# Memory keys loaded by tokens instead of by heads, in a hybrid decoder layer

## Chip, core and metric

The kernel runs on one core of a Trainium2 chip. The metric is the device time of one execution in microseconds (us), as the median of several runs. Beside it stands one execution taken by the hardware profiler, whose rows are read here. Engines are named as the profile names them: PE (matrix multiplications; PEld its weight loads), DVE (vector engine), ACT (scalar engine), POOL, and SP, which here only issues DMAs. DMAs are carried out by 16 DMA engines that all queues share.

## What is computed

One layer of a decoder serves a prompt of 512 tokens and, with the same weights, eight samples of four tokens each. Three sub-layers follow each other: a mixer (an mLSTM group and a differential-attention group), cross-attention into 256 memory tokens, and a gated MLP with a short convolution. The change lies in the cross-attention of the samples, whose keys and values come from a cache:

```
def mem_attend(h, mk, mv, w_mq, w_mo):
    B, T, _ = h.shape
    q = (h @ w_mq).reshape(B, T, MEM_HEADS, MEM_HEAD_DIM)
    s = jnp.einsum('bqhd,bkhd->bhqk', q.astype(jnp.float32), mk.astype(jnp.float32)) * (MEM_HEAD_DIM ** -0.5)
    p = jax.nn.softmax(s, axis=-1)
    o = jnp.einsum('bhqk,bkhd->bqhd', p, mv.astype(jnp.float32)).reshape(B, T, D_MODEL)
    return o.astype(h.dtype) @ w_mo
```

For the samples `mk` and `mv` are `cache_mem_k` and `cache_mem_v`, of shape (1, 8, 256, 4, 256): eight samples, 256 tokens, four heads of 256 numbers. In memory a token's four heads lie behind each other (4 KB), and one head of one token is a piece of 1 KB. Keys and values are 8.4 MB each, all in float32.

## The kernel before

The whole layer is one program for one core. A scheduler places the instructions of all engines by its own estimate of their times, and each engine then runs its instructions strictly in that order. Nearly all loads are issued by SP, one behind the other. Weights come in slots of a ring (`wslot`, tag `W`, four buffers) by way of a staging ring (`wst`, six buffers).

The stage around the change is the projection of queries with `w_mq` and the attention behind it:

- `gemmB(hqT, ...)` multiplies `w_mq` in eight column blocks. The first four run as two halves of columns (matmuls at L472), the last four block by block (L485). Each block ends with an evacuation from PSUM: ACT writes `qh` (L1420), DVE the rest `ql` (L1421), and ACT the samples' queries `qs` (L1423). Five PSUM buffers serve these products in turn.
- POOL spreads `qs` into `qx` (L1408), a matrix with the queries of one head in each row group.
- `mk_load(b)` loads the keys of sample b (L1493): two halves of 128 tokens, each into a tile of 128 partitions by 1024 columns. Partition 32 h + t holds head h; column 256 k + d holds number d of token 32 k + t. The tiles are staging buffers (`wst`) for three samples, weight slots (`kvt`, free when a block of the projection is done) for four, and one extra tile.
- `mk_turn(b)` transposes each tile in blocks of 32 by 32 on DVE (L1498), so that the head's dimension lies on partitions.
- `mk_scores` multiplies them with `qx` on PE (L1510), for the samples 0, 2, 4, 6 first and 1, 3, 5, 7 later, between pieces of the prompt's own cross-attention (L1441, L1459, L1471). The sums, the softmax and the values' product (`mv_out`, L1548) follow. The values are loaded (`mv_load`, L1538) into the buffers that the scores have given back.
- Behind that SP loads the convolution's rows (`cr`) and `w_mo`, and PE goes on with the output projection and the MLP.

At L1766 and L1767, in the MLP, a tile `cvr` is stored to two outputs. The prediction uses these stores for comparison: the first takes 8 partitions of 128 numbers to 2 rows with 4 blocks each, the second 64 partitions to 16 rows with 4 blocks each. At L1775 a store of 16 partitions goes to 16 rows.

Of the kernel before, what the change touches and what calls it, by code (L numbers as in the profile page):

```python
# [15 lines left out]
P = 128  # L16
# [4 lines left out]
NS = NB * TS  # L21
ROWS = SEQ + NS
H = 4
# [54 lines left out]
def kernel(ctx: ExitStack, tc: tile.TileContext, I, O):  # L78
# [29 lines left out]
    def T2(shape, name, dt=F32):  # L108
        return t2p.tile(list(shape), dt, name=name, tag="T2")
# [17 lines left out]
    def v2(t, b):  # L127
        return t.rearrange("p (a b) -> p a b", b=b)
# [10 lines left out]
    dma = nc.sync.dma_start  # L139
# [69 lines left out]
    def stage():  # L209
        return stg.tile([P, 1024], F32, name="wst", tag="st")  # L210
# [319 lines left out]
    for b in range(2):  # L530
        kept.append(norm_turn(xms[b], P, "g_mem_src", memT, b * P))
        if b == 0:

            t = turned[0].ins
            fill = mmp("fill")
            for _ in range(NFILL):
                with burst(t):
                    t = mm(fill, lhsT=warm[:, 0:P], rhs=warm, start=True, stop=True).ins
# [132 lines left out]
    for c0, c1 in HALF:  # L671
# [5 lines left out]
        t = T2([64, n], "gt")  # L677
# [253 lines left out]
    for g in range(2):  # L931
        for h in range(0, H, 2):
            t = stage().rearrange("p (j b e) -> p j b e", j=2, b=4)
# [38 lines left out]
    t = None  # L972
    for h in range(H):
        with burst(t):
            t = mm(pg[NS * h:NS * h + NS, P:2 * P + 1], lhsT=sm_t[:, h, :], rhs=vNs[:, h, :], start=True, stop=True).ins
    for h in range(H):
        with burst(t):
            t = mm(pg[NS * h:NS * h + NS, 4:12], lhsT=qT[:, h, SEQ:], rhs=nT[:, h, :], start=True, stop=True).ins
    for b in range(NB):
        for h in range(H):  # L980
            with burst(t):
                t = mm(pi[NS * h:NS * h + NS, 0:P], lhsT=qzm[:, 256 * h + b * NS:256 * h + (b + 1) * NS],
                       rhs=csts[b // 4, h][:, b % 4, :], start=(b == 0), stop=(b == NB - 1)).ins
# [226 lines left out]
    for b in range(4):  # L1210
        c = slice(b * P, b * P + P)
# [3 lines left out]
    kst, kts, pts, aTs, outs, rcs = {}, {}, {}, {}, {}, {}  # L1215
# [260 lines left out]
    kst, vts = {}, {}  # L1476
# [4 lines left out]
    def two(i):  # L1481

        if i < 3:
            return [stage(), stage()]
        t = wp.tile([P, 2, DM], F32, name="kvt", tag="W") if i < 7 else S([P, 2, DM], F32, "kvt")
        return [t[:, 0], t[:, 1]]

    def mk_load(b):

        kst[b] = two(home[b])  # L1490
        for c in range(2):
            for h in range(H):
                dma(out=v2(kst[b][c][NS * h:NS * h + NS], 256),  # L1493
                    in_=I["cache_mem_k"][0, b, c * P:(c + 1) * P, h].rearrange("(k t) d -> t k d", t=NS))

    def mk_turn(b):
        for t in kst[b]:
# [2 lines left out]
    def mk_scores(bs):  # L1500

        t = None
        for b in bs:
            ps = mmp("ssc")[:, :256]
            for c in range(2):
                kv = kst[b][c].rearrange("p (k j t) -> p k j t", j=8, t=NS)
                for j in range(8):
                    g = NS * (j % 4)
                    with burst(t):
                        t = mm(v2(ps[g:g + NS, c * P:c * P + P], NS), lhsT=qx[:, j, b // 2 * 2:b // 2 * 2 + 2].rearrange("p n r -> p (n r)"),  # L1510
                               rhs=kv[:, :, j, :], start=(j < 4), stop=(j >= 4)).ins
            nc.scalar.copy(out=sc[:, b], in_=ps)
        return t
# [40 lines left out]
    for k in range(4):  # L1554
        mk_load(SEQS[k])
    for i, _ in enumerate(gemmB(hqT, [ev_q(m) for m in range(4, 8)])):
        if i % 4 == 1:
            mk_turn(SEQS[i // 4])
        if i % 4 == 3:
            mk_load(SEQS[4 + i // 4])  # L1560
# [11 lines left out]
    t = mk_scores(SEQS[4:])  # L1572
# [205 lines left out]
    for gi, js in enumerate(groups):  # L1778
# [8 lines left out]
        def one(b, ps, i, s, cs=slice(0, 512)):  # L1787
            t = act[i // 2][:, i % 2]
            st, en = i == 0, i == nk - 1
            if b == 4:  # L1790
                return sample_mm(ps, [acs[i], acs[i + 1]], s[1], i == 0, i == nk - 2)
            s = s[0]
            c0 = b * P
            mm(ps, lhsT=t[:, 0, c0:c0 + P], rhs=s[:, 0, i % 2, cs], start=st, stop=False)  # L1794
            mm(ps, lhsT=t[:, 0, c0:c0 + P], rhs=s[:, 1, i % 2, cs], start=False, stop=False)  # L1795
            return mm(ps, lhsT=t[:, 1, c0:c0 + P], rhs=s[:, 0, i % 2, cs], start=False, stop=en)  # L1796
# [29 lines left out]
        if not last:  # L1826
            behind = []
            for n0 in (0, 512):
# [4 lines left out]
                for i in range(nk):  # L1833
# [3 lines left out]
                    for b in range(4):  # L1837
                        t = one(b, ps[b], i, s)
# [14 lines left out]
        def chunk(b, n0):  # L1853
            while len(wd) < (nk // 2 if n0 == 0 else nk):
                wd.append(W.get())
            w = 256 if (b, n0) == (TORD[-1], 512) else 512
            for o in range(0, 512, w):
                ps = mmp()[:, :w]
                for i in range(0, nk, 2 if b == 4 else 1):
                    t = one(b, ps, i, wd[(n0 and nk // 2) + i // 2], slice(o, o + w))  # L1860
                add_y(b, ps, n0 + o, w)
            return t
# [39 lines left out]
        t = chunk(TORD[1], 0)  # L1902

        for n0 in (0, 512):
            with burst(t.ins):
                t = chunk(TORD[0], n0)
# [78 lines left out]
```

## Time and profile before

| | |
|---|---|
| median of 3 runs | 952.89 us (952.66 to 952.95) |
| the profiled execution | 950.42 us |
| its span, first to last instruction | 948.6 us |
| mean granted clock of PE | 0.990 |
| PE busy | 918.3 us (97%) |
| DVE, ACT, POOL busy | 606.2, 377.7, 202.6 us |
| moved by DMA | 130.30 MB, 137 GB/s on average |

A row of a timeline has the start in us from the span's beginning, the duration, engine, line, operation, output and inputs with their shapes, the count of merged instructions, and in brackets the idle time of the engine before it and what ended it. A row of waits has who waited for whom, the total in us, how often, and the longest. The DMA share in a row by stretch is the mean busy share of the 16 DMA engines; transfers that were begun in a stretch count whole, so that it can exceed 1. PEclk is the clock that PE was granted, as a share of full speed.

### The profile page before, as it was taken

How to read it: one execution, taken by the hardware profiler on the slowest of the kernel's cores; microseconds unless marked ns; L12 is line 12 of the kernel's file. 1: busy time of each engine (PE TensorE's matmuls, PEld its weight loads, DVE VectorE, ACT ScalarE, POOL GpSimd, SP SyncE). 2: the span in 40 equal slices, each digit the busy share in tenths (PEclk: the TensorE clock that was granted, in tenths of full speed). 3: DMA queues.
4: the chain of work that ended last, by engine and by line, in shares of the span. 5: the costliest groups of instructions: out<-in, count | busy, mean ns of one | idle time of the engine just before them, and what ended most of it. 6: DMA issues, size and time to landing. Idle time of an engine off the chain costs nothing. (4 is left out here: it accounts for less than half of the span.)

```text
span 948.6 us, 17140 instructions
## 1 busy us (share of the span) xinstructions
PE 918.3 (97%) x6612; PEld 800.8 (84%) x6612; DVE 606.2 (64%) x1120; ACT 377.7 (40%) x727; POOL 202.6 (21%) x401
## 2 busy tenths in 40 slices
PE   8999999999999999988989999999999999999995
PEld 5899787889866778988767899989988997999974
DVE  6845145565886358576544778638757775676767
ACT  5655234344676357613434532322212222222232
POOL 6610000115432226301000544001110110110114
PEclk9999999999999999999989999999999999999998
DMA  8950023344870539999744733062053313512023
GB/s 285 309 183 2 2 88 137 89 139 131 280 245 9 176 103 343 262 192 260 273 175 124 208 126 89 25 174 72 8 142 100 102 27 92 153 49 89 24 93 116
DMA packets 127586, 130.30 MB, mean 137 GB/s; under 512 B 9336, under 2 KB 95193, under 8 KB 127505
## 3 DMA queue, kind: packets, MB, share of 16 engines
q1 hardware_dynamic: 121320, 125.70, 43.8%
q10 hardware_dynamic: 6184, 3.52, 1.2%
q8 instruction: 52, 0.85, 0.4%
q14 instruction: 30, 0.24, 0.1%
HBM read 112.26 MB, written 16.93 MB: 136 GB/s over the span
## 5 line engine op out<-in xcount | busy, mean ns | idle before, releaser
L485 PE MATMUL mm<-fT,wslot 128*128 128x256 f32 x1872 | 235.9, 288 | 0.0
L485 PEld LDWEIGHTS mm<-fT,wslot 128*128 128x128 f32 x1872 | 234.4, 188 | 1.8 <-issue 0.8
L146 ACT CAST wslot<-wst 128x1024 fp32r<-128x1024 f32 x125 | 130.7, 1050 | 256.7 <-issue 71.8
L147 DVE TENSOR_TENSOR wslot<-wst,wslot 128x1024 fp32r<-128x1024 f32 x125 | 155.2, 1246 | 83.3 <-ACT wslot L146 82.8
L1795 PE MATMUL mm<-wslot,act 128*128 128x512 f32 (+1 forms) x180 | 70.2, 391 | 0.0
L1796 PE MATMUL mm<-wslot,act 128*128 128x512 f32 (+1 forms) x180 | 70.0, 392 | 0.0
L1794 PE MATMUL mm<-wslot,act 128*128 128x512 f32 (+1 forms) x180 | 69.3, 387 | 0.0
L1700 POOL COPY cvo<-u 128x2 f32<-128x2 f32 x43 | 10.4, 243 | 204.0 <-DVE u L1698 194.0
L411 PE MATMUL mm<-wslot,hT 128*128 128x512 f32 x128 | 51.3, 402 | 0.0
L485 PE MATMUL mm<-hT,wslot 128*128 128x256 f32 (+1 forms) x384 | 51.0, 289 | 0.0
L413 PE MATMUL mm<-wslot,hT 128*128 128x512 f32 x128 | 51.0, 399 | 0.0
L412 PE MATMUL mm<-wslot,hT 128*128 128x512 f32 x128 | 50.8, 397 | 0.0
L1695 DVE TENSOR_TENSOR u<-mm,rsb 128x256 f32<-128x256 f32 x43 | 18.1, 423 | 50.1 <-PE mm L485 50.1
L485 PEld LDWEIGHTS mm<-hT,wslot 128*128 128x128 f32 x384 | 49.2, 188 | 0.5 <-issue 0.2
L1794 PEld LDWEIGHTS mm<-wslot,act 128*128 128x128 f32 x180 | 34.3, 191 | 8.0 <-issue 0.8
L1796 PEld LDWEIGHTS mm<-wslot,act 128*128 128x128 f32 x180 | 33.8, 188 | 7.3 <-issue 0.4
L1795 PEld LDWEIGHTS mm<-wslot,act 128*128 128x128 f32 x180 | 33.8, 188 | 7.2
L1712 ACT ACTIVATE c<-c 128x560 f32<-128x560 f32 x21 | 14.1, 672 | 57.0 <-DVE c L1706 57.0
L1706 DVE SCALAR_TENSOR_TENSOR c<-u,cvT,c 128x560 f32<-128x560 f32 x43 | 34.3, 797 | 0.9
L1705 DVE SCALAR_TENSOR_TENSOR c<-u,cvT,c 128x560 f32<-128x560 f32 x43 | 34.1, 793 | 0.2
L1807 DVE TENSOR_TENSOR yp<-mm,yp 128x512 f32<-128x512 f32 (+1 forms) x41 | 27.2, 674 | 5.2 <-PE mm L1796 5.1
L485 PE MATMUL mm<-hqT,wslot 128*128 128x256 f32 x192 | 26.2, 299 | 3.8 <-ACT qs L1423 3.8
(482 smaller groups left out, 1828.4 us busy)
## 6 DMA issues: line engine op xcount, KB each, us to landing
wst<-in_w_up_dram SPq DMA_DIRECT2D x42, 512.0 KB
wst<-in_w_in_dram SPq DMA_DIRECT2D x28, 512.0 KB
wst<-in_w_down_dram SPq DMA_DIRECT2D x20, 512.0 KB
kvt<-in_cache_mem_k_dram SPq DMA_DIRECT2D x40, 128.0 KB
kvt<-in_cache_mem_v_dram SPq DMA_DIRECT2D x10, 512.0 KB
wst<-in_w_mk_dram SPq DMA_DIRECT2D x8, 512.0 KB
xb<-in_x_prompt_dram SPq DMA_DIRECT2D x8, 512.0 KB
wst<-in_cache_dk_dram SPq DMA_DIRECT2D x16, 256.0 KB
```

Source lines behind the costliest of these rows:

```text
L146: nc.scalar.copy(out=hi, in_=src)
L147: (eng or nc.vector).tensor_tensor(out=lo, in0=src, in1=f32(hi), op=SUB)
L411: mm(ps[b], lhsT=xt.hi(k, c0, c0 + n), rhs=s[:, 0, kk, :], start=(k == 0), stop=False)
L412: mm(ps[b], lhsT=xt.hi(k, c0, c0 + n), rhs=s[:, 1, kk, :], start=False, stop=False)
L413: return mm(ps[b], lhsT=xt.lo(k, c0, c0 + n), rhs=s[:, 0, kk, :], start=False, stop=(k == nk - 1))
L485: mm(ps[i], lhsT=s[:, l, k, :], rhs=x(k, c0, c1), start=(k == 0 and j == 0), stop=(k == 7 and j == 2))
L1705: STT(out=c, in0=u[:, 1:EXT - 1], scalar=w[1], in1=c, op0=MUL, op1=ADD)
L1706: STT(out=c, in0=u[:, 0:EXT - 2], scalar=w[0], in1=c, op0=MUL, op1=ADD)
L1794: mm(ps, lhsT=t[:, 0, c0:c0 + P], rhs=s[:, 0, i % 2, cs], start=st, stop=False)
L1795: mm(ps, lhsT=t[:, 0, c0:c0 + P], rhs=s[:, 1, i % 2, cs], start=False, stop=False)
L1796: return mm(ps, lhsT=t[:, 1, c0:c0 + P], rhs=s[:, 0, i % 2, cs], start=False, stop=en)
L1807: VTT(out=y, in0=ps, in1=y, op=ADD)
```

## The change

A half of a sample's keys still takes four transfers of 128 pieces of 1 KB, and the tile ends up with the same content. Before, a transfer took one head of all 128 tokens and wrote 32 partitions, four pieces in each. Now it takes 32 tokens with all four heads and writes all 128 partitions, one piece in each.

```
     def mk_load(b):

         kst[b] = two(home[b])
         for c in range(2):
-            for h in range(H):
-                dma(out=v2(kst[b][c][NS * h:NS * h + NS], 256),
-                    in_=I["cache_mem_k"][0, b, c * P:(c + 1) * P, h].rearrange("(k t) d -> t k d", t=NS))
+            for k in range(4):
+                dma(out=kst[b][c][:, 256 * k:256 * k + 256], in_=I["cache_mem_k"][0, b, c * P + NS * k:c * P + NS * k + NS].rearrange("t h d -> h t d"))
```

In the built program the two sides of a transfer have these dimensions, slowest first: before, 32 tokens × 4 × 256 numbers in the source and 32 partitions × 4 × 256 in the destination; now 4 heads × 32 tokens × 256 in the source and 128 partitions × 1 × 256 in the destination. The new code is one line shorter, so the lines behind it are numbered one less (L1498 becomes L1497).

The scheduler also places a few instructions anew. On SP, from the last of the `w_mq` loads on, there stood (kvt and wst from cache_mem_k are the keys, from cache_mem_v the values, cr the convolution's rows; a count at the end stands for equal rows merged):

```order
L1493 DMA kvt<-in_cache_mem_k_dram 32x4x256 x3
L1493 DMA wst<-in_cache_mem_k_dram 32x4x256 x8
L1493 DMA kvt<-in_cache_mem_k_dram 32x4x256 x5
L1493 DMA wst<-in_cache_mem_k_dram 32x4x256 x16
L1493 DMA kvt<-in_cache_mem_k_dram 32x4x256 x16
L1607 DMA cr<-in_state_conv_dram 16x896
L1493 DMA kvt<-in_cache_mem_k_dram 32x4x256 x8
```

and now stands:

```order
L1493 DMA kvt<-in_cache_mem_k_dram 128x1x256 x2
L1493 DMA wst<-in_cache_mem_k_dram 128x1x256 x8
L1493 DMA kvt<-in_cache_mem_k_dram 128x1x256 x4
L1493 DMA wst<-in_cache_mem_k_dram 128x1x256 x4
L1493 DMA kvt<-in_cache_mem_k_dram 128x1x256 x2
L1493 DMA wst<-in_cache_mem_k_dram 128x1x256 x12
L1493 DMA kvt<-in_cache_mem_k_dram 128x1x256 x16
```

The keys of the extra tile (the first kvt) now alternate with those of the staging buffers in other portions; the 64 transfers stay in one piece ahead of the values.

On DVE, in the last part of the projection, the transposes of keys stand between the evacuations `ql`. Before:

```order
L1421 SCALAR_TENSOR_TENSOR ql<-mm,qh 128x256 x2
L1498 STREAM_TRANSPOSE kvt<-kvt 128x1024 x2
L1421 SCALAR_TENSOR_TENSOR ql<-mm,qh 128x256 x2
L1444 TENSOR_REDUCE cnm<-sca 128x2 x2
L1498 STREAM_TRANSPOSE kvt<-kvt 128x1024
L1448 RECIPROCAL csu<-csu 128x2 x2
L1450 TENSOR_SCALAR cp<-cp,csu 128x256 x4
L1498 STREAM_TRANSPOSE kvt<-kvt 128x1024
```

Now:

```order
L1421 SCALAR_TENSOR_TENSOR ql<-mm,qh 128x256 x2
L1497 STREAM_TRANSPOSE kvt<-kvt 128x1024
L1444 TENSOR_REDUCE cnm<-sca 128x2 x2
L1497 STREAM_TRANSPOSE kvt<-kvt 128x1024
L1448 RECIPROCAL csu<-csu 128x2 x2
L1450 TENSOR_SCALAR cp<-cp,csu 128x256 x4
L1497 STREAM_TRANSPOSE kvt<-kvt 128x1024
```

One of the transposes has moved from ahead of the last `ql` to behind it, so three stand there instead of two. The other places that moved, on PE, DVE and ACT around the convolution's coefficients (`cvT`), lie behind the values' product.

## The prediction

> **What bounds the kernel now.** I read the page first, then busy times by stretch around the memory keys, then the timelines of PE, DVE and SP there, then the DMA rows.
>
> ```profile
> span 948.6 us, 17140 instructions
> PE 918.3 (97%) x6612; PEld 800.8 (84%) x6612; DVE 606.2 (64%) x1120; ACT 377.7 (40%) x727; POOL 202.6 (21%) x401
> ```
>
> PE is busy in all but 30 us of the span, so a faster stage can win only what PE idles in it, while a slower transfer in front of PE costs its whole delay. The stage in question is 393 to 449 us. From the view by stretch (busy time of PE, PEld, DVE, ACT, POOL, then granted clock, busy share of the 16 DMA engines, rate):
>
> ```profile
> core 0: us, PE busy (x) PEld busy (x) DVE busy (x) ACT busy (x) POOL busy (x), PEclk, DMA share, GB/s
> 390.00:393.00 3.00, 3.00 (x26) 3.00 (x25) 1.07 (x3) 1.61 (x3) 2.26 (x2) 1.00 1.03 286
> 409.00:413.00 4.00, 1.03 (x7) 0.62 (x5) 4.00 (x5) 1.42 (x3) 0.91 (x4) 1.00 0.52 141
> 413.00:417.00 4.00, 3.20 (x15) 3.20 (x16) 3.11 (x5) 0.95 (x4) 0.51 (x3) 0.66 0.65 158
> 421.00:425.00 4.00, 4.00 (x34) 4.00 (x34) 1.98 (x2) 0.66 (x2) 0.00 (x0) 1.00 1.14 215
> 461.00:465.00 4.00, 4.00 (x30) 3.40 (x32) 3.35 (x11) 2.10 (x7) 0.00 (x0) 1.00 1.02 419
> ```
>
> The first is w_mq (512 B pieces into 128 partitions), the fourth the keys (1 KB pieces, 32 partitions per transfer), the last the values (4 KB pieces, 128 partitions). All sixteen engines are full in all three, yet the keys move 215 GB/s, half the values' rate and less than w_mq with pieces half as long. The piece's size doesn't explain that; the 32 partitions may. [...]
>
> What the slow keys cost, from the timelines of DVE and PE (start, duration, and in brackets the idle time before and who ended it):
>
> ```profile
> 403.45 1.25 DVE L1498 STREAM_TRANSPOSE wst<-wst 128x1024 f32<-128x1024 f32 x1 [6.71 <-DMA wst<-in_cache_mem_k_dram]
> ...
> 442.26 1.23 DVE L1498 STREAM_TRANSPOSE kvt<-kvt 128x1024 f32<-128x1024 f32 x1
> ```
>
> ```profile
> 403.51 6.15 PE L485 MATMUL mm<-hqT,wslot 128*128 128x256 f32 x48
> 410.07 0.38 PE L485 MATMUL mm<-hqT,wslot 128*128 128x256 f32 x1 [0.41 <-ACT qs L1423]
> 413.80 19.65 PE L485 MATMUL mm<-hqT,wslot 128*128 128x288 f32 x143 [3.35 <-ACT qs L1423]
> ...
> 438.71 3.57 PE L1510 MATMUL ssc<-wst,qx 128*32 128x128 f32 x95 [2.42 <-POOL qx L1408]
> ...
> 445.22 3.70 PE L1510 MATMUL ssc<-kvt,qx 128*32 128x128 f32 x128
> ...
> 469.63 4.52 PE L1548 MATMUL pso<-kvt,caz 128*32 128x256 f32 x80
> ```
>
> DVE runs in order, and its transposes of keys stand between the evacuations ql (L1421). While it waits 6.71 us for keys, the evacuations behind it wait, then qs on ACT, then the PSUM buffers, and PE stops for 0.41 + 3.35 us, later for 2.42 us (POOL's qx waits for qs). After the stop the clock is 0.66, and 143 matmuls take 19.65 us where 48 took 6.15: 19.65 − 143 × 0.128 = 1.3 us. So at most 7.5 us can be won here.
>
> **The change part by part.** Bytes, pieces and the layout in SBUF stay: 64 transfers, each 128 pieces of 1 KB. What changes is how one is written down. Before, both sides begin with 32 (tokens, partitions). After, the destination is 128 partitions and the source is 4 heads × 32 tokens. One other transfer of this kernel has two sides cut unequally like that, the store of cvr (L1766: 8 partitions to 2 rows × 4 blocks of 512 B; L1767: 64 to 16 × 4). L1775 is a like store with equal sides. Their SP rows and the keys' (duration min/median/max in ns):
>
> ```profile
> L1766 SPq DMA_DIRECT2D out_dram<-cvr x10: 644/656/767, 593.6 to 905.6; - x10
> L1767 SPq DMA_DIRECT2D out_dram<-cvr x10: 591/597/646, 594.4 to 906.2; - x10
> L1775 SPq DMA_DIRECT2D out_dram<-cvr x4: 314/321/341, 712.1 to 714.2; - x4
> L1493 SPq DMA_DIRECT2D kvt<-in_cache_mem_k_dram x40: 311/398/1568, 392.9 to 437.8; - x40
> ```
>
> So the first cost: an issue takes 0.60 to 0.66 us instead of 0.32, as bounds of what a key's issue takes. 64 × 0.65 = 42 us, about what the keys' issues last now.
>
> The second is larger. The DMA view of the 1.2 us of one L1766 and the 1 us of the L1767 behind it, and of the whole stretch of keys, counts the packets:
>
> ```profile
> DMA packets 10, 0.00 MB, mean 3 GB/s; under 512 B 2, under 2 KB 10, under 8 KB 10
> DMA packets 80, 0.03 MB, mean 33 GB/s; under 512 B 16, under 2 KB 80, under 8 KB 80
> DMA packets 11353, 9.61 MB, mean 200 GB/s; under 512 B 1097, under 2 KB 11313, under 8 KB 11349
> ```
>
> Beside its data each transfer has a few tiny packets: 10 − 8 = 2 for L1766, 80 − 64 = 16 for L1767, and 1097 over 68 or so transfers, 16 each, for the keys. I read them as one completion mark per DMA engine that took part: a store whose sides begin with 8 and 2 ran on two engines, one with 64 and 16 on sixteen. A number that divides both sides fits all three (2; 16; 16 for 32 and 32). For 128 and 4 it gives four. [...]
>
> So I expect each key transfer on four engines, 32 pieces each. Whether on the same four every time the rows don't show; I take the same, the simpler reading, and keep four in turn among the rivals. The price of a 1 KB piece: bounds are the values' row, 419 / (16 × 1.02) = 25.7 GB/s per engine, and the keys' row now, 215 / (16 × 1.14) = 11.8. Between them lies the one other transfer in 1 KB pieces, the last stores of the kernel (946.15 to 947.2 us, two of 128 × 256):
>
> ```profile
> q1 hardware_dynamic: 288, 0.26, 74.5%
> ```
>
> 16 × 1.05 × 0.745 = 12.5 us of engine time for 256 pieces and 32 marks, 0.391 us per eight pieces and a mark. I take this one, because it has the size and all partitions. Thirty-two pieces: 4 × 0.391 = 1.56 us per transfer. The stream is then 64 × 1.56 = 100.1 us (8.39 MB at 84 GB/s); by the bounds 82 us (4 × 25.7 GB/s) and 178 us (4 × 11.8).
>
> When it starts and when it is issued (DMA view of 394 to 396 us and 396.3 to 398.3 us; SP's timeline; waits of DVE and SP, with us in total, times, longest):
>
> ```profile
> q1 hardware_dynamic: 892, 0.45, 85.2%
> q1 hardware_dynamic: 651, 0.46, 118.1%
> ```
>
> ```profile
> 392.94 2.52 SPq L1493 DMA_DIRECT2D kvt<-in_cache_mem_k_dram  x3
> ...
> 434.19 4.02 SPq L1493 DMA_DIRECT2D kvt<-in_cache_mem_k_dram  x8
> 440.24 0.83 SPq L1538 DMA_DIRECT2D wst<-in_cache_mem_v_dram  x2
> ...
> 458.58 1.57 SPq L1538 DMA_DIRECT2D kvt<-in_cache_mem_v_dram  x2
> ```
>
> ```profile
> DVE wst L1498 <- DMA wst<-in_cache_mem_k_dram: 10.5, 4, 6.7
> DVE kvt L1498 <- DMA kvt<-in_cache_mem_k_dram: 7.0, 6, 2.4
> ...
> SPq L1493 <- DMA kvt<-in_cache_mem_k_dram: 5.0, 16, 0.6
> ```
>
> Until 396 the queue moves 0.45 MB / 892 = 0.5 KB pieces, all w_mq; then the average grows, so keys begin at about 396.3. Eight semaphores serve SP's transfers in turn (the last row), so eight are in flight, 12 us of work: SP doesn't starve the engines. The last key's buffer needs the last projection slot, which PE frees long before the transfer's turn.
>
> **The sum.** Last data at 396.3 + 100.1 = 496.4. Landing: the last packets of the kernel lie before 947.2, the span ends at 948.6, so 1.4 us (an estimate): 497.8. The last transpose 1.2 us, then the last sample's quarter of the 128 score matmuls, 3.70 / 4 = 0.9: 499.9. Now these matmuls end at 445.22 + 3.70 = 448.9. That is +51.0 us, all of it on the path, since the softmax over keys, the value matmuls and everything behind wait for the last score. The gemm before it is paced by the keys too but ends earlier: its last evacuation stands ahead of the last three transposes, each of four transfers, so some 3 × 4 × 1.56 = 19 us before the end of the stream. Cold clock after the long waits: +1.3, as above. Together +52.3.
>
> The values come next on SP. Sixteen transfers, 8.4 MB at 419 GB/s, are 20 us; on the four late engines they start at 496.4 and land at about 518, and the second batch of value matmuls is due at 469.63 + 51.0 = 520.6. Hidden, by 3 us; without that cover some 3 us. The conv rows and w_mo behind them shift along. The reorderings on DVE and PE around cvT (L1623) are work with cover: nothing.
>
> 950.42 (the profiled execution) + 52.3 = 1002.7; the median of the runs, 952.89, is 2.5 higher, so 1005 on that scale. By the bounds of the price: 82 us of stream give 987, 178 us give 1083.
>
> **Rivals.** First, two of the four engines get in each other's way. They would start 32 partitions apart and go through them in step; before, the engines all wrote into one block of 32 and had 11.8 GB/s each. In step throughout, the upper bound holds: 1083; partly, 1030 to 1060. For it: equal pieces from the same start. Against: w_mq leaves the engines up to 2 us apart (the mixed stretch above). [...]
>
> Second, on the other side: all sixteen engines take part, or different fours in turn. Then pieces go to all partitions, engine time falls to 64 × 0.39 = 25 us, and SP's issue decides, 64 × (0.65 + 0.05) = 45 us, as now (392.94 to 438.2). The keys of the first samples land a little sooner; of the 7.5 us some 0 to 7 are won, 946 to 953. For it: 215 against 419 GB/s. Against: the two marks of L1766. It decides if the marks over the keys stay at about 1,100.
>
> Third, only the values are late, by a few us more: 1005 to 1010, inside the first case.
>
> **How the numbers follow.** Four engines at 40 to 62 ns per piece, 987 to 1035: 0.72. Four engines in each other's way, above that: 0.18. Sixteen: 0.10, of it 0.06 faster and 0.04 the same. A measurement tells a change from none at about 0.2%, 2 us. The range from 985 to 1045 holds the first case and half of the second's lower part, about 0.8.
>
> **What would show it.** In the changed profile: tiny packets over the keys at about 4 per transfer (some 300 in all, not 1,100); a DMA share near 0.25 and 80 to 90 GB/s from 397 to 495 us; issues of 0.6 us and more; DVE idle before L1497 (the transposes, one line up) of 50 to 70 us in all instead of 10.5 + 7.0; the second score batch ending near 500. A share of 0.25 at 50 GB/s is the first rival. Shares near 0.5 and above with 16 marks each make the prediction wrong, and so does PE running through this stage without waits.

## The result, and the profile after

The changed kernel took 1001.25 us (median of 4 runs, 1000.65 to 1003.05), the kernel before beside it 952.92 us (4 runs, 952.66 to 955.1): a ratio of 1.0505, 95% interval 1.0485 to 1.0525. It is slower by 48.3 us; forecast were 1005 us in a range of 985 to 1045. The profiled execution of the changed kernel took 1003.05 us with a span of 1001.3.

The page's head and the view by stretch (columns as before: busy time of PE, PEld, DVE, ACT, POOL, granted clock, share of the 16 DMA engines, rate):

```profile
span 1001.3 us, 17142 instructions
PE 928.7 (93%) x6612; PEld 809.3 (81%) x6612; DVE 604.4 (60%) x1120; ACT 376.8 (38%) x727; POOL 199.6 (20%) x401
```

```profile
390.00:393.00 3.00, 3.00 (x26) 3.00 (x26) 2.07 (x4) 2.27 (x5) 2.71 (x2) 1.00 1.12 316
413.00:417.00 4.00, 0.00 (x0) 0.00 (x0) 2.28 (x3) 0.00 (x0) 0.00 (x0) 0.81 0.27 89
421.00:425.00 4.00, 0.00 (x0) 0.00 (x0) 0.05 (x1) 0.00 (x0) 0.00 (x0) 0.50 0.28 89
496.00:500.00 4.00, 2.98 (x48) 2.71 (x48) 2.12 (x6) 3.22 (x11) 0.00 (x0) 1.00 1.02 398
```

The same 1 KB pieces that moved at 215 GB/s with a share of 1.14 now move at 89 GB/s with 0.27 to 0.28. Neither the DMA engines' busy time nor the bytes grew (SP's queue took 43.8% of the sixteen engines' time in 948.6 us before and 40.2% in 1001.3 us now; 130.30 MB moved in both): close to three quarters of the sixteen engines' time in the two rows is idle. In w_mq ahead of the keys (first row, 1.12) and the values behind them (last row, 1.02) the share is full as before. PE does nothing at all in the second and the third row, and its clock falls to 0.50.

The counts of packets over the keys, SP's issues, and who waited for keys (total, times, longest):

```profile
DMA packets 10628, 9.70 MB, mean 101 GB/s; under 512 B 310, under 2 KB 10546, under 8 KB 10623
```

```profile
L1493 SPq DMA_DIRECT2D kvt<-in_cache_mem_k_dram x40: 561/1379/1832, 393.3 to 484.1; - x40
```

```profile
DVE kvt L1497 <- DMA kvt<-in_cache_mem_k_dram: 36.3, 9, 5.1
DVE wst L1497 <- DMA wst<-in_cache_mem_k_dram: 32.2, 6, 8.9
```

310 tiny packets instead of 1097: between four and five per key transfer, with those of neighbouring transfers among them. An issue takes at least 0.561 us instead of 0.311; the median of 1.379 is mostly waiting, since SP goes at the transfers' pace of one per 1.47 us (worked out below). By 438.1 us it has issued 32, and since the first piece at 396.9 the data of (438.1 − 396.9) / 1.47 = 28 have moved, so about four are in flight. DVE waits 68.5 us for keys, where it waited 17.5.

What that does to PE (start, duration, count, idle time before and who ended it), with the last transposes on DVE:

```profile
427.92 8.31 PE L485 MATMUL mm<-hqT,wslot 128*128 128x288 f32 x48 [8.85 <-ACT qs L1423]
...
453.13 7.60 PE L485 MATMUL mm<-hqT,wslot 128*128 128x288 f32 x47 [3.33 <-DVE ql L1421]
...
477.58 4.56 PE L1509 MATMUL ssc<-wst,qx 128*32 128x128 f32 x96 [11.01 <-POOL qx L1408]
...
497.01 1.08 PE L1509 MATMUL ssc<-kvt,qx 128*32 128x128 f32 x32 [1.13 <-issue]
...
517.35 4.52 PE L1547 MATMUL pso<-kvt,caz 128*32 128x256 f32 x80
...
532.13 0.69 PE L1594 MATMUL ost<-cpk,oS 128*128 128x128 f32 x2 [6.39 <-ACT oS L1591]
```

```profile
480.98 1.25 DVE L1497 STREAM_TRANSPOSE kvt<-kvt 128x1024 f32<-128x1024 f32 x1 [3.98 <-DMA kvt<-in_cache_mem_k_dram]
486.86 1.25 DVE L1497 STREAM_TRANSPOSE kvt<-kvt 128x1024 f32<-128x1024 f32 x1 [3.46 <-DMA kvt<-in_cache_mem_k_dram]
494.43 1.25 DVE L1497 STREAM_TRANSPOSE kvt<-kvt 128x1024 f32<-128x1024 f32 x1 [5.10 <-DMA kvt<-in_cache_mem_k_dram]
```

The releasers named on PE are qs, ql and qx, not a DMA: the chain is keys, transpose on DVE, evacuation ql behind it in DVE's order, then qs and qx, then PE. The last score ends at 497.01 + 1.08 = 498.1 instead of 448.9, +49.2 us. The values' product stands 47.7 us later than before, the next product that needs it (ost) 50.7 later.

### The profile page after: what moved, and what is told of

Same layout as the page of the kernel before. It is cut to its first block, busy times and chain, and to the rows that moved or that the text cites. A ratio compares the mean times of both kernels' runs of the same rounds, so it can differ in the third digit from the quotient of the medians.

```text
span 1001.3 us, 17142 instructions
## 1 busy us (share of the span) xinstructions
PE 928.7 (93%) x6612; PEld 809.3 (81%) x6612; DVE 604.4 (60%) x1120; ACT 376.8 (38%) x727; POOL 199.6 (20%) x401
## 2 busy tenths in 40 slices
DMA packets 126817, 130.30 MB, mean 130 GB/s; under 512 B 8567, under 2 KB 94424, under 8 KB 126736
## 3 DMA queue, kind: packets, MB, share of 16 engines
q1 hardware_dynamic: 120552, 125.69, 40.2%
## 4 chain that ended last, share of the span: by engine, by line
PE 70%; DMA 9%; SPq 7%; DVE 7%; ACT 3%; issue 2%; POOL 2%; DVEq 0%; ACTq 0%; POOLq 0%
PE mm L485 28%; SPq L1493 7%; PE mm L411 5%; PE mm L412 5%; PE mm L413 5%; PE mm L1794 3%; PE mm L1795 3%; PE mm L1793 3%; PE mm L472 3%; DMA kvt<-in_cache_mem_k_dram 2%; PE sda L1257 2%; DMA x_d<-xb 2%; DVE wslot L147 1%; PE mm L390 1%; DVE xb L1166 1%
## 5 line engine op out<-in xcount | busy, mean ns | idle before, releaser
L485 PE MATMUL mm<-hqT,wslot 128*128 128x256 f32 x192 | 31.1, 331 | 25.1 <-ACT qs L1423 16.6
L485 PEld LDWEIGHTS mm<-hqT,wslot 128*128 128x128 f32 x192 | 30.0, 229 | 26.1 <-ACT qs L1423 17.2
L485 PEld LDWEIGHTS mm<-hT,wslot 128*128 128x128 f32 x384 | 49.2, 188 | 0.5 <-issue 0.2
L1694 DVE TENSOR_TENSOR u<-mm,rsb 128x256 f32<-128x256 f32 x43 | 18.2, 424 | 50.3 <-PE mm L485 50.3
L1705 DVE SCALAR_TENSOR_TENSOR c<-u,cvT,c 128x560 f32<-128x560 f32 x43 | 34.3, 798 | 0.9
L1497 DVE STREAM_TRANSPOSE kvt<-kvt 128x1024 f32<-128x1024 f32 x10 | 12.5, 1246 | 36.6 <-DMA kvt<-in_cache_mem_k_dram 36.3
```

What stands on the lines that cost most here:

```text
L485: mm(ps[i], lhsT=s[:, l, k, :], rhs=x(k, c0, c1), start=(k == 0 and j == 0), stop=(k == 7 and j == 2))
L1705: STT(out=c, in0=u[:, 0:EXT - 2], scalar=w[0], in1=c, op0=MUL, op1=ADD)
```

## The experiments

Each edit below is against the changed kernel, or, where it says so, against the kernel before. For all of them the stretch from 400 to 408 us is compared, where only keys are loaded, but for up to two packets of instructions (one of 16 KB before and after). By stretch and by packets it read, first before and then after:

```profile
400.00:408.00 8.00, 8.00 (x64) 8.00 (x63) 3.27 (x3) 1.33 (x2) 0.00 (x0) 1.00 1.05 219
```

```profile
DMA packets 1905, 1.75 MB, mean 219 GB/s; under 512 B 213, under 2 KB 1904, under 8 KB 1904
```

```profile
400.00:408.00 8.00, 8.00 (x64) 8.00 (x63) 1.25 (x1) 1.33 (x2) 0.00 (x0) 1.00 0.28 91
```

```profile
DMA packets 720, 0.73 MB, mean 91 GB/s; under 512 B 22, under 2 KB 719, under 8 KB 719
```

Tiny packets per transfer of 128 pieces: before 213 / ((1905 − 213) / 128) = 16.1, after 22 / ((720 − 22) / 128) = 4.0. The theory from the prediction, the author's reading of the tiny packets there, is that a transfer runs on a number of engines that divides the first dimension of both sides, four for 128 and 4. Rivals: something about 128 partitions in 1 KB pieces is slow, or engines disturb each other.

### One cut changed at a time

In the following four kernels a transfer still fills 128 partitions with one piece of 1 KB each, from the same 128 KB of the cache. Only how the source is written down differs, and with it its first dimension beside the destination's 128: 128 (whole16), 16 (cut16), 8 (cut8), 2 (cut2).

**whole16**:

```
-    in_=I["cache_mem_k"][0, b, ...].rearrange("t h d -> h t d")
+    in_=I["cache_mem_k"][0, b, ...].rearrange("t h d -> (t h) d")
```

> The same 128 KB per transfer into the same 128 partitions, but as 128 pieces in the order in which they lie in memory, so that both sides are cut into 128. The keys' pieces land in other partitions, so the samples' cross-attention is computed from permuted keys; all instructions are the same. Theory A (number of engines): 16 marks per transfer, DMA share near 1, 300 to 400 GB/s over the keys, issues back at 0.3 to 0.5 us; PE's waits of 0.41, 3.35 and 2.42 us and the cold clock of 1.3 us go: 944 to 948 us. Theory B (1 KB pieces into 128 partitions are slow by themselves): stays at about 1000 us. Theory C (SP's issue of an unequal cut is what takes 1.4 us): also 944 to 948, so C is told apart by the next three.

Measured: 944.44 us (944.25 to 946.98), 0.9915 of the kernel before (0.9891 to 0.9939). The stretch, its packets, SP's issues (least, median and longest in ns) and PE's timeline:

```profile
400.00:408.00 8.00, 8.00 (x65) 8.00 (x64) 6.21 (x6) 2.75 (x5) 0.91 (x4) 1.00 0.73 226
```

```profile
DMA packets 1955, 1.80 MB, mean 226 GB/s; under 512 B 216, under 2 KB 1953, under 8 KB 1953
```

```profile
L1493 SPq DMA_DIRECT2D kvt<-in_cache_mem_k_dram x40: 351/430/1652, 393.0 to 432.4; - x40
```

```profile
411.00 18.11 PE L485 MATMUL mm<-hqT,wslot 128*128 128x288 f32 x143 [1.27 <-ACT qs L1423]
...
438.43 3.70 PE L1510 MATMUL ssc<-kvt,qx 128*32 128x128 f32 x128
```

128 partitions in 1 KB pieces are not slow here: with 16 marks per transfer (216 × 128 / 1739 = 15.9) the loss is gone and 8.6 us are won (5.8 to 10.4 by the interval); the prediction had named 7.5 as the most there is to win. The scores end at 442.1, 6.8 sooner than before. The rate was expected at 300 GB/s and more with full engines and is 226 at a share of 0.73: the engines now wait for SP, whose 64 issues from 393.0 to 432.4 are 0.62 us apart. For 7.7 of these 39.4 us SP itself waits, mostly for buffers that DVE and PE haven't given back, so the issue alone isn't shown to be the limit here.

**cut16**, **cut8** and **cut2** write the same rows as `a` groups, each of every `a`-th row (with a = 4 it would be the change itself):

```
+    src = I["cache_mem_k"][0, b, ...].rearrange("t h d -> (t h) d")
-    in_=I["cache_mem_k"][0, b, ...].rearrange("t h d -> h t d")
+    in_=src.rearrange("(r a) d -> a r d", a=16)     # a=8 in cut8, a=2 in cut2
```

> Source cut into 16 x 8 pieces, destination 128 partitions: as unequal as the change, but 16 divides both. Pieces land in permuted partitions as in whole16. Theory A: 16 marks per transfer, share about 0.6 at 190 to 210 GB/s because SP's issue takes 0.6 to 0.7 us each, keys done after some 45 us: 945 to 953 us. Theory B: about 1000 us. Theory C: issues of 1.4 us, about 1000 us.

> Source cut into 8 x 16 pieces. Permuted partitions as above. Theory A: 8 marks per transfer, share about 0.5, 178 GB/s, 47 us of keys: 951 to 960 us. Theories B and C: about 1000 us.

> Source cut into 2 x 64 pieces. Permuted partitions as above. Theory A: 2 marks per transfer, share 0.13, 45 GB/s, 188 us of keys, 94 us more than in the changed kernel: about 1095 us. Theories B and C: about 1000 us.

Measured: cut16 950.87 us (948.95 to 952.78), 0.9974 of before (0.9962 to 0.9987); cut8 957.41 us and cut2 1094.69 us, one run each. Of cut16 the stretch, SP's issues and the second batch of scores:

```profile
400.00:408.00 8.00, 8.00 (x64) 8.00 (x63) 4.58 (x4) 1.33 (x2) 0.00 (x0) 1.00 0.54 164
```

```profile
L1494 SPq DMA_DIRECT2D kvt<-in_cache_mem_k_dram x40: 542/597/1857, 392.7 to 438.9; - x40
```

```profile
444.00 3.70 PE L1510 MATMUL ssc<-kvt,qx 128*32 128x128 f32 x128
```

Of cut8 the stretch, the packets and the same scores:

```profile
400.00:408.00 8.00, 8.00 (x64) 8.00 (x64) 2.71 (x3) 1.33 (x2) 0.00 (x0) 1.00 0.55 180
```

```profile
DMA packets 1482, 1.44 MB, mean 180 GB/s; under 512 B 88, under 2 KB 1481, under 8 KB 1481
```

```profile
448.50 3.81 PE L1510 MATMUL ssc<-kvt,qx 128*32 128x128 f32 x128
```

Of cut2 the stretch and the packets:

```profile
400.00:408.00 8.00, 8.00 (x65) 8.00 (x64) 0.00 (x0) 1.33 (x2) 0.00 (x0) 1.00 0.14 47
```

```profile
DMA packets 354, 0.37 MB, mean 47 GB/s; under 512 B 5, under 2 KB 353, under 8 KB 353
```

Marks per transfer: 88 × 128 / 1394 = 8.1 and 5 × 128 / 349 = 1.8. Rates: 47, 91 and 180 GB/s where the marks (1.8, 4.0, 8.1) tell of two, four and eight engines. Without the marks and the packet of instructions they are 348, 697 and 1393 pieces of 1 KB in 8 us, or 44.5, 89.2 and 178.3 GB/s: 22.3 GB/s per engine in all three. With 2, 4 and 8 as the source's first dimension (cut2, after, cut8) the rate is proportional to it, at the same partitions and bytes. That settles the cause in these kernels: how many engines take part, and that the way the sides are cut sets it. In all three the number is also the smaller of the two sides' first dimensions, so no run here tells a common divisor from a minimum. The proportion also answers the first rival: four engines get as much each as two or eight, so they do not hold each other up.

Between cut16 and whole16 the number of marks is about the same (150 × 128 / (1415 − 150) = 15.2 and 15.9); the cut differs, and with it some places that the scheduler gave to instructions on SP and DVE. An issue takes 0.54 us at least instead of 0.35, the rate is 164 GB/s instead of 226, and the time 6.4 us longer. In cut16 SP waits for others only 2.1 us, and its issues are 0.73 us apart (392.7 to 438.9). So the way a side is written down costs at SP as well, where sixteen engines wait for work; how much of the 6.4 us the other places have is not divided.

### Are they always the same four?

**four_two_queues** issues every second key transfer of the changed kernel from ACT's queue, **two_queues** does the same with the heads 2 and 3 of the kernel before:

```
-                dma(out=kst[b][c]...
+                (nc.scalar.dma_start if k % 2 else dma)(out=kst[b][c]...     # before: if h > 1
```

> The changed kernel with every second transfer issued by ACT. If transfers on four engines always run on the same four, whichever queue issues them: share 0.25 to 0.3, 89 GB/s, 996 to 1008 us. If the other queue gets other engines: share 0.5, about 178 GB/s, 953 to 962 us.

> The kernel before with heads 0 and 1 issued by SP, heads 2 and 3 by ACT, so that each DMA engine has two queues with targets in different halves of the partitions. [...] Rival: ACT's issues (some 32 of 0.4 us and their waits) stand ahead of its evacuations of qh and qs and PE waits for those: 953 to 962 us.

Measured: four_two_queues 1000.14 us (one run). two_queues 954.66 us (952.84 to 956.67), 1.0026 of before (1.0006 to 1.0047). The stretch and the queues of the first (q1 is SP's, q10 ACT's):

```profile
400.00:408.00 8.00, 4.57 (x35) 4.35 (x33) 0.00 (x0) 1.33 (x2) 0.00 (x0) 1.00 0.27 89
```

```profile
q1 hardware_dynamic: 454, 0.45, 17.0%
q10 hardware_dynamic: 261, 0.26, 9.9%
```

Two queues together get 17.0 + 9.9 = 26.9% of the engines, just what one got (27.0). Had the second queue used another four, the share would have grown towards 0.5. So the same four serve both queues, transfer after transfer; which of the sixteen they are no run here shows. In two_queues the 64 issues are shared, yet the time is not better. No gain in rate came either: it is 202 GB/s in this stretch, against 219 before. As the rival said, evacuations on ACT now stand behind its issues: a `qh` (L1420) begins at 400.72 us, after 9.8 us in which ACT computed nothing and issued two transfers in 5.4 us.

**mixed** loads the first half of each sample by heads and the second by tokens:

```
             for k in range(4):
+                if c == 0:
+                    dma(out=v2(kst[b][c][NS * k:NS * k + NS], 256),
+                        in_=I["cache_mem_k"][0, b, c * P:(c + 1) * P, k].rearrange("(k t) d -> t k d", t=NS))
+                    continue
                 dma(out=kst[b][c][:, 256 * k:256 * k + 256], ...
```

> The first half of each sample's keys comes by heads as before (32 partitions per transfer), the second half by tokens as in the changed kernel, 32 transfers of each kind in turn. Theory A (a transfer by tokens lies on the same four engines always, one by heads on all sixteen, the four among them): the four engines carry both, 32 x 1.47 us (from the changed kernel's transposes, 5.9 us per four transfers) + 32 x 0.59 us (before: 64 transfers in about 38 us) = 66 us; last data at 396.3 + 66 = 462, scores end near 466 instead of 448.9: +17, about 970 us; DMA share about 0.6 and 127 GB/s. Rival (work is spread so that the twelve other engines take over): 4.2 MB at 215 GB/s beside 4.2 MB at 89 GB/s, 47 us, which ends at 443, about as the issue does: 953 to 957 us.

Measured: 979.9 us (978.43 to 982.22), 1.0273 of before (1.0247 to 1.0299). The transposes of three second halves, two us by stretch, and the second batch of scores:

```profile
445.99 1.25 DVE L1501 STREAM_TRANSPOSE kvt<-kvt 128x1024 f32<-128x1024 f32 x1 [5.24 <-DMA kvt<-in_cache_mem_k_dram]
...
454.92 1.25 DVE L1501 STREAM_TRANSPOSE kvt<-kvt 128x1024 f32<-128x1024 f32 x1 [5.85 <-DMA kvt<-in_cache_mem_k_dram]
...
463.46 1.25 DVE L1501 STREAM_TRANSPOSE kvt<-kvt 128x1024 f32<-128x1024 f32 x1 [5.51 <-DMA kvt<-in_cache_mem_k_dram]
```

```profile
450.00:452.00 2.00, 0.00 (x0) 0.00 (x0) 0.00 (x0) 0.00 (x0) 0.00 (x0) 1.00 0.85 152
452.00:454.00 2.00, 0.00 (x0) 0.00 (x0) 0.00 (x0) 0.00 (x0) 0.00 (x0) 1.00 0.27 84
```

```profile
474.71 3.70 PE L1513 MATMUL ssc<-kvt,qx 128*32 128x128 f32 x128
```

The rival, in which twelve engines run ahead and nothing is lost, is out: the engines swing between nearly all and four, and a sample takes 8.5 to 8.9 us. That is more than the 4 × 1.47 + 4 × 0.59 = 8.2 of the expectation, and the scores end at 478.4, 29.5 later than before and not 17. So the direction was right and the size 10 us too small. Part of it is in these rows: eight samples at 8.7 us are 70 instead of 66, and the whole second batch of scores (128 matmuls, 3.7 us) now lies behind the last key, where the sum had a quarter. The rest I haven't divided.

### Does the number of partitions set an engine's rate?

Before, an engine got 219 / (16 × 1.05) = 13.0 GB/s while it was busy; after, 91 / (16 × 0.28) = 20.3. **half64** takes one head of 128 tokens to 64 partitions, in two pieces each, with transfers taking turns between partitions 0 to 63 and 64 to 127; **half64_pairs** sends two in a row to each half:

```
-            for k in range(4):
-                dma(out=kst[b][c][:, 256 * k:256 * k + 256], ...
+            for h in range(H):
+                g, m = 64 * (h % 2), 512 * (h // 2)     # half64_pairs: 64 * (h // 2), 512 * (h % 2)
+                dma(out=v2(kst[b][c][g:g + 64, m:m + 512], 256),
+                    in_=I["cache_mem_k"][0, b, c * P:(c + 1) * P, h].rearrange("(k t) d -> t k d", t=64))
```

> Still one head of 128 tokens per transfer, but into 64 partitions (0 to 63 or 64 to 127) with two pieces each; keys land in other partitions, so the samples' cross-attention is computed from permuted keys. Both sides begin with 64, so 16 engines. [...] Rival (what counts is the number of partitions): price per engine near 20 GB/s, share well below 1, then the issue of about 0.6 us decides: 946 to 951 us.

> As half64 (one head of 128 tokens into 64 partitions, two pieces each; the samples' cross-attention is again computed from keys in permuted places), but two transfers in a row go to partitions 0 to 63 and two to 64 to 127, instead of taking turns. [...] If a unit cut of 64 is as slow as one of 32, 12 GB/s per engine: share 0.9 and more at 190 GB/s or less. Time within 2 us of half64's 953.4.

Measured, one run each: 953.44 and 953.29 us. By stretch, half64 and half64_pairs:

```profile
400.00:408.00 8.00, 8.00 (x64) 8.00 (x63) 3.17 (x3) 1.33 (x2) 0.00 (x0) 1.00 0.59 165
```

```profile
400.00:408.00 8.00, 8.00 (x65) 8.00 (x64) 3.77 (x4) 1.33 (x2) 0.00 (x0) 1.00 0.64 174
```

165 / (16 × 0.59) = 17.5 and 174 / (16 × 0.64) = 17.0 GB/s per busy engine, against 13.0 with 32 partitions and 226 / (16 × 0.73) = 19.3 with 128. An engine gets more with more partitions per transfer, but these two runs do not tell why: transfers to both halves are in flight together in either order, and SP, whose issues are 0.74 us apart (394.2 to 440.9 in half64), sets the rate, not the engines. The price per engine is nearer to the 20 GB/s expected if the number of partitions counts than to the 12 of a cut into 32, though half64's 953.4 us lies above the 946 to 951 that went with the 20.

**order0213** keeps the kernel before and issues the heads in another order, so that neighbours in the queue write partitions 64 apart:

```
-            for h in range(H):
+            for h in (0, 2, 1, 3):
```

> The kernel before with the heads in the order 0, 2, 1, 3, so that neighbouring transfers write different halves of the partitions. If all engines go through the transfers in step, nothing changes: 215 GB/s, 952 to 954 us. If engines drift apart by a transfer, two halves are written at once: 250 GB/s and more, 945 to 951 us.

Measured: 950.16 us (948.15 to 953.1), 0.9974 of before (0.9957 to 0.9992), and so the fastest here of those that leave every key in its place; it beats both kernels. In this stretch the rate is 208 GB/s at a share of 0.87, 14.9 GB/s per busy engine instead of 13.0; PE's two waits on the way to the scores are

```profile
PE mm L485 <- ACT qs L1423: 3.3, 1, 3.3
PE ssc L1510 <- POOL qx L1408: 1.2, 1, 1.2
```

instead of 3.8 and 2.4. The gain is small, though the interval leaves out 1. The time lies where the second case of the expectation had it, but that case's 250 GB/s did not come (208), so why the order helps isn't shown.

## Why the prediction was right

**Issue.** Forecast 0.60 to 0.66 us, measured at least 0.56, a little under these bounds; as forecast, it lies beside the slower transfers and costs nothing. Its price shows only between cut16 and whole16. That unequal sides are its cause, as the step took from the stores of cvr, is not borne out: in half64 both sides begin with 64, and an issue takes 0.60 us at least:

```profile
L1494 SPq DMA_DIRECT2D kvt<-in_cache_mem_k_dram x40: 596/605/1612, 394.2 to 440.9; - x40
```

What sets an issue's time stays open. The prediction's eight transfers in flight did not hold for the changed kernel either: it had about four, and long issues in place of waits between them. What followed from it did hold, since SP kept the four engines busy (a share of 0.27 to 0.28).

**Four engines, always the same.** Read from two rows of tiny packets and confirmed by the counts (1.8, 4.0, 8.1 and 15.9 marks in cut2, after, cut8, whole16), by rates in the same proportion over the first three (44.5, 89.2, 178.3 GB/s), and by the second queue (26.9% against 27.0%). "The same every time" had been an assumption; four_two_queues shows it.

**The price of a transfer.** Forecast 1.56 us from the rate of the last stores. The transposes come 486.86 − 480.98 = 5.9 us apart, four transfers each, 1.47 us: at this pace the stream takes 94 us, not 100.1, at 89 GB/s instead of 84, so the price was 6 us too large over the whole. From the first piece at 396.9 to the end of the last at 493.5 the stream took 96.6 us. The last transpose, due at 497.8, began at 494.43, so only 3.4 us of that arrived. Most of the rest lies in the last gap: from 486.86 to 494.43 are 7.6 us instead of 5.9. In that time the values already move beside the last keys, for the share is no longer that of four engines:

```profile
486.00:490.00 4.00, 1.31 (x6) 1.32 (x7) 2.47 (x7) 0.19 (x1) 0.00 (x0) 0.64 0.70 201
```

That the values slow the last keys is likely, but no run tests it. One slip in the prediction changes nothing: 62 ns per piece would be 127 us of stream and 1032 us, not 1035.

**The end of the scores.** Forecast 499.9, measured 498.1: +49.2 instead of +51.0. That the whole delay lies on the path holds in every variant, within 3 us:

| | scores end, against before (us) | median, against the before beside it (us) |
|---|---|---|
| whole16 | −6.8 | 944.44 − 953.05 = −8.6 |
| cut16 | −1.2 | 950.87 − 953.05 = −2.2 |
| cut8 (one run) | +3.4 | 957.41 − 953.05 = +4.4 |
| cut2 (one run) | +143.1 | 1094.69 − 953.05 = +141.6 |
| four_two_queues (one run) | +49.7 | 1000.14 − 952.12 = +48.0 |
| two_queues | +2.5 | 954.66 − 952.12 = +2.5 |
| mixed | +29.5 | 979.9 − 953.14 = +26.8 |
| half64 (one run) | 0.0 | 953.44 − 952.12 = +1.3 |
| half64_pairs (one run) | −0.1 | 953.29 − 953.14 = +0.2 |
| order0213 | −0.9 | 950.16 − 952.12 = −2.0 |
| after | +49.2 | 1001.25 − 952.92 = +48.3 |

**The clock.** Forecast +1.3 us for the cold clock. PE's busy time grew by 10.4 us (918.3 to 928.7) with the same matmuls, so the cold clock cost far more work time than that: 48 matmuls from 427.92 us on took 8.31 us at a granted clock of 0.72, where 48 took 6.15 at 1.00 (from 403.51 us before). But most of it lies in a stage that goes at the keys' pace, where a slower matmul is hidden. A term of its own behind the scores can't be read from the medians (48.3 against 49.2).

**Values, conv rows and w_mo.** The values were hidden from PE, as forecast: the value product starts 47.7 us later, no more than the scores. That the rows behind them "shift along" was too simple. The cast of w_mo on ACT and its issue on SP, first before and then after:

```profile
477.49 2.24 ACT L146 CAST wslot<-wst 128x1024 fp32r<-128x1024 f32 x2 [5.95 <-PE cpo L1471]
```

```profile
470.94 3.10 SPq L231 DMA_DIRECT2D wst<-in_w_mo_dram  x6
```

```profile
529.53 1.04 ACT L146 CAST wslot<-wst 128x1024 fp32r<-128x1024 f32 x1 [10.26 <-issue]
```

```profile
521.19 3.79 SPq L231 DMA_DIRECT2D wst<-in_w_mo_dram  x6
```

w_mo is issued 50.3 us later and its casts start 52.0 later; the copy oS stands behind the casts on ACT, and ost on PE waits 6.39 us for it instead of 3.38. In the profiled pair that is 3 us behind the values' product. But cut8 has the same 6.39 us at this place with keys only 3.4 us late, and whole16 has 5.02 us with keys that come sooner than before. So late values aren't shown to be the reason, and it stays open.

**The sum.** The profiled pair differs by 1003.05 − 950.42 = 52.6 us, the medians by 48.3; the sum said 52.3. The profiled execution after is the longest of its four runs, and the one before lies under all its timed runs, so the sum's near agreement with the pair is partly luck: the scores' term was 1.8 us too large, and the rest of the difference between pair and medians is spread from run to run.

**The rivals.** Engines in each other's way: out, 22.3 GB/s per engine (89 / 4) with four engines, as much as with two. No run shows engines that hinder each other in part, from which this rival had its 1030 to 1060 us; in its place the trace has 89 GB/s for the four together. Sixteen engines or fours in turn: out, by 4 marks and a share of 0.28. The values' lateness: no wait of PE for values in the changed kernel.

## What to carry to other kernels

Before changing how a transfer is cut, write down the slowest dimension of both sides as the built instruction has them: here, with 128 on the destination's side, a source that begins with 2, 4, 8 or 128 gave 1.8, 4.0, 8.1 and 15.9 marks per transfer and 47, 91, 180 and 226 GB/s, so 128 partitions on the one side did not help when the other began with 4. In a profile, the sign of it here was a DMA share of 0.27 to 0.28 under a long wait, with 4.0 tiny packets per transfer. Once the marks tell of sixteen engines, look at SP next: with transfers of 128 KB on one queue, its issues and the buffers that they wait for, 0.62, 0.73 and 0.74 us apart, were the limit that followed in whole16, cut16 and half64.

## What the runs showed of the hardware

- One DMA engine moved 22.3 GB/s in 1 KB pieces whether two, four or eight of them worked by the marks (cut2, after, cut8: 44.5, 89.2 and 178.3 GB/s). With sixteen (15.9 marks) in whole16, SP's issues, 0.62 us apart with their waits for buffers, came first (226 GB/s at a share of 0.73).
- SP's issue of 128 pieces of 1 KB into `kvt` took 0.31 us at least as 32 × 4 on both sides, 0.35 as 128 on both, 0.54 as 16 × 8 against 128 and 0.60 as 64 × 2 on both. Equal sides alone did not make the issue short.
- Two queues with four-engine transfers shared the same four engines in four_two_queues (26.9% of engine time together, 27.0% with one).
- A busy engine got 13.0, 17.0 to 17.5 and 19.3 GB/s with 32, 64 and 128 partitions per transfer. What sets it was not separated from the issue, which was the limit with 64 and part of it with 128.
